# Logits asked for chunk by chunk in the value steps, and inverse row sums stored from their column form

## The chip, the cores and the metric

The kernel runs on one core of a Trainium2 chip. The metric is the device time of one execution in microseconds (us). Before the change three runs took 1028.32, 1027.87 and 1028.21 us; their median is 1028.21.

## The reference

One layer of a decoder trunk over 1024 tokens of width 1024, in float32: a combined projection, a pooling mixer on half of the width, attention with a forgetting gate on the other half (8 heads of 64), an output projection, a layer norm, a squared-relu MLP of width 4096 and a second layer norm. The change lies in the attention:

```python
log_f = jax.nn.log_sigmoid(f_logit)            # per token and head
cf = jnp.cumsum(log_f, axis=-1)
s = einsum('bhqd,bhkd->bhqk', q, k) * HEAD_DIM ** -0.5
s = s + cq[..., :, None] - cf[..., None, :]
s = where(kpos <= qpos, s, NEG_INF)            # causal
p = softmax(s, axis=-1)
out = einsum('bhqk,bhkd->bhqd', p, v)
x = layer_norm(ALPHA * x + concat(pool, attn) @ w_out)
```

## The kernel before, in words

Every float32 product is made from operands split in a high and a low part, so that most products are three matmuls (L82, L83, L84). The program runs in stages: the projections for values and gate, pooling and the first queries and keys; then attention (about 100 to 330 us), into whose steps the next projections and the first output projections are mixed as filling; then the rest of the output projection; then the MLP, which reads its weights from DRAM and is a dense run of matmuls (L796, L1136) to the end.

**Units.** Attention works in 32 units `(p, e, m)`: head pair p, head e of the pair, and block m of 256 queries, which is two row blocks of 128 queries. For the first three pairs a head's units come as m = 3, 2, 1, 0; for the last pair m rises and the two heads alternate. A unit has two halves. `att_probs` makes the probabilities of a unit: per row block the logits in chunks of up to 512 keys (two matmuls at L375 into a PSUM bank with the tag `s`, of which there are three), a fused add-and-minimum on VectorE that takes the chunk out of the bank (L380, with a running minimum `nm`), and one exponential over the row block on ScalarE (L382), which also leaves the row sums in `rsum`. A row block with up to 512 keys has one chunk, one with more has two; units with m = 2 or 3 thus have four chunks, those with m = 0 or 1 two. `att_values` uses the probabilities: for each of its m + 1 value steps `jp` it turns four (in the last step three) 128x128 blocks by TensorE transposes (L405, into a bank with the tag `pt`, of which there are two), splits them out of the bank (L406 on ScalarE, L407 on VectorE) and, up to two steps later, multiplies them with the values (L420, into halves of the one `pv` bank). After a unit's last product the result is added up in a tile `mx` (L429, L430; the `U` tiles, two slots) and stored to `mix_dram` by SyncE's queue (L432, L434).

**What sets the order.** `att_probs` is a generator, and `att_values` of one unit drives `att_probs` of the next (`ahead`). Before the change the generator yields once per row block. It is asked for one row block in step `jp == 0`, and for all that is left in step `min(m, (m + 1) // 2 + 1)`, which is the last step for every m. After each step `fillstep` lets in a share of the filling. A scheduler then places the instructions on each engine; each engine works in its order.

**Inverse row sums.** When the sums of a head (first three pairs) or of a row pair (last pair) are there, VectorE takes their reciprocal into a column tile `ri` of 128 partitions and 8 or 2 columns (L443). `row_scales`, called at the unit's last product, turns it: a TensorE transpose into a `pt` bank (L466), a copy to a row tile (L468, ScalarE), and a store to `rin_dram` (L469, SyncE's queue) of 8 or 2 rows of 512 bytes. It happens 6 times with 8 columns and 8 times with 2. `attention_part` later loads the inverses broadcast over 64 partitions (L580) and multiplies them in (L584).

Of the kernel before, what the change touches and what calls it, by code (L numbers as in the profile page):

```python
# [14 lines left out]
P = 128  # L15
S = 1024
D = 1024
NT = S // P
# [18 lines left out]
def trunk(ctx, tc, xT, xn, wuqk, wvf, bf, poolw, pscale, wout, g1, b1, w1, w2, g2, b2, out):  # L37
# [5 lines left out]
    nc = tc.nc  # L43
# [7 lines left out]
    def slot(tag, shape, dt=F32R):  # L51
        uid[0] += 1
        return sb.tile([P] + list(shape), dt, tag=tag, bufs=NBUF[tag], name=f"{tag}{uid[0]}")

    def small(shape, tag, dt=F32, bufs=1, pool=None):
        uid[0] += 1
        return (pool or sb).tile(list(shape), dt, tag=tag, bufs=bufs, name=f"{tag}_{uid[0]}")
# [5 lines left out]
    def bank(tag=None):  # L63
        uid[0] += 1
        if tag is None:
            tag = CYCLE[rr[0] % 8]
            rr[0] += 1
        return ps.tile([P, CH], F32, tag=tag, bufs=PBUF[tag], name=f"{tag}{uid[0]}")
# [18 lines left out]
    ident = small([P, P], "ident")  # L87
# [17 lines left out]
    rin_dram = dr.tile([NH, S], F32, name="rin_dram")  # L105
# [96 lines left out]
    for t in range(4, NT):  # L202
        for half in range(2):
            b = bank()[:, 0:VW]
# [53 lines left out]
    def run(gen):  # L258
        for _ in gen:
            pass  # L260
# [86 lines left out]
    def gate_row(h):  # L347
        if h not in gate_rows:
            gate_rows[h] = slot("A", [S], F32)
            rsum[h] = small([P, NT], "rsum", bufs=3)  # L350
            nc.sync.dma_start(gate_rows[h], ncf_dram[h : h + 1, :].to_broadcast([P, S]))

    def att_probs(p, e, m, prob):


        KS, q = QK[p][0][e], QK[p][1]
        h = 2 * p + e
        gate_row(h)
        nb = gate_rows[h]
        falling = p < NPAIR - 1  # L360
        for i in (2 * m + 1, 2 * m) if falling else (2 * m, 2 * m + 1):
            nk = (i + 1) * P
            n2 = nk if m % 2 else 256 * (m + 1)
            qs = slice(i * P, (i + 1) * P)
            if falling:
                nc.gpsimd.tensor_tensor(nb[:, qs], nb[:, qs], maskb, ALU.add)
            prob[i % 2] = pt = slot("A", [S], F32)
            top = BIG
            for a in range(0, nk, CH):
                b = min(n2, a + CH)  # L370
                diag = not falling and a <= i * P < b
                sp = bank("s")[:, : b - a]
                for n in range(2):
                    rows = q[n, e, i // 4][:, i % 4 * P : (i % 4 + 1) * P]
                    nc.tensor.matmul(sp, rows, KS[:, a:b], start=n == 0, stop=n == 1 and not diag)  # L375
                if diag:
                    nc.tensor.matmul(sp[:, i * P - a : (i + 1) * P - a], identb, maskb, start=False, stop=True)
                b = min(nk, b)
                nm = small([P, 1], "nm", bufs=8)
                nc.vector.tensor_tensor_reduce(pt[:, a:b], sp[:, : b - a], nb[:, a:b], -1.0, top, ALU.add, ALU.min, nm)  # L380
                top = nm
            nc.scalar.activation(pt[:, :nk], pt[:, :nk], AF.Exp, bias=nm, scale=-1.0, accum_out=rsum[h][:, i : i + 1])  # L382
            yield

    def att_values(p, e, m, prob, ahead):
        h = 2 * p + e
        rows = slice(e * HD, (e + 1) * HD)
        orow = slice((1 - e) * HD, (2 - e) * HD)
        if "values" not in fill:
            fill["values"] = bank("pv")  # L390
        ov = fill["values"][:, 256 * fill["half"] : 256 * fill["half"] + 256]
        fill["half"] = 1 - fill["half"]

        def turned(jp):
            tp = bank("pt")
            tt = slot("A", [2, CH])
            if jp < m:
                blocks = [(jj * 256 + ii * P, 2 * jp + jj, ii) for jj in range(2) for ii in range(2)]
                ev = slice(0, CH)
            else:  # L400
                blocks = [(P, 2 * jp + 1, 1), (2 * P, 2 * jp, 0), (3 * P, 2 * jp, 1)]
                ev = slice(P, CH)
                nc.gpsimd.memset(tt[:, :, 0:P].bitcast(F32), 0.0)
            for col, j, ii in blocks:
                fill["turn"] = nc.tensor.transpose(tp[:, col : col + P], prob[ii][:, j * P : (j + 1) * P], ident).ins  # L405
            nc.scalar.copy(tt[:, 0, ev], tp[:, ev])  # L406
            fill["sub"] = nc.vector.tensor_tensor(tt[:, 1, ev], tp[:, ev], tt[:, 0, ev].bitcast(F32), ALU.subtract).ins  # L407
            return tt

        def multiply(jp, tt):  # L410
            mov = ((0, 256), (256, CH)) if jp < m else ((256, CH), (0, 256))
            with ExitStack() as order:
                for behind in (fill["piece"], fill["turn"]):
                    if behind:
                        order.enter_context(tc.issue_after(behind))
                for s in range(2):
                    for jj in range(2):
                        j = 2 * jp + jj
                        a, b = mov[jj]
                        nc.tensor.matmul(  # L420
                            ov, V[j][:, h].rearrange("p s d -> p (s d)"), tt[:, s, a:b],
                            start=(j == 0 and s == 0), stop=(j == 2 * m + 1 and s == 1),
                        )
            if jp == m:
                last = p == NPAIR - 1
                if not last or e == 0:
                    fill["mx"] = slot("U", [256], F32)
                mx = fill["mx"]
                nc.scalar.copy(mx[rows], ov[orow])  # L429
                nc.vector.tensor_tensor(mx[rows], ov[rows], mx[rows], ALU.add)  # L430
                if not last:
                    nc.sync.dma_start(mix_dram[m, rows, NG + p, :], mx[rows])  # L432
                elif e:
                    nc.sync.dma_start(mix_dram[m, :, NG + p, :], mx)  # L434
                if last:
                    row_scales(h, 2 * m, 2)
                elif m == 0:
                    row_scales(h, 0, NT)

        if p == NPAIR - 1 or m == 0:  # L440
            ri = small([P, NT], "ri", bufs=3)
            i, n = (2 * m, 2) if p == NPAIR - 1 else (0, NT)
            nc.vector.reciprocal(ri[:, :n], rsum[h][:, i : i + n])  # L443
            inverse[h, i] = ri

        for jp in range(m + 1):
            left.append((multiply, jp, turned(jp)))
            if jp == 0:
                fill["last"] = fill["sub"]
                next(ahead, None)  # L450
            if jp == min(m, (m + 1) // 2 + 1):
                run(ahead)
            fillstep()
            values(2)

    left, inverse = [], {}

    def values(n):
        while len(left) > n:
            step, jp, tt = left.pop(0)  # L460
            step(jp, tt)

    def row_scales(h, i, n):
        ri = inverse.pop((h, i))
        tp = bank("pt")
        nc.tensor.transpose(tp[0:n, 0:P], ri[:, :n], ident)  # L466
        row = small([NT, P], "row")
        nc.scalar.copy(row[0:n], tp[0:n, 0:P])  # L468
        nc.sync.dma_start(rin_dram[h, i * P : (i + n) * P].rearrange("(i q) -> i q", q=P), row[0:n])  # L469

    g0 = qk_proj(0)
    for _ in range(2 * KT):
# [222 lines left out]
    def fillstep():  # L695
        fill["credit"] += fill["rate"]
        while fill["credit"] >= 1.0:
            fill["credit"] -= 1.0
            piece = next(fill["gen"], None)
            if piece and fill["pieces"] < 8:  # L700
                fill["piece"], fill["pieces"] = piece, fill["pieces"] + 1
# [4 lines left out]
    for n, unit in enumerate(order):  # L706
# [20 lines left out]
        if n % 8 == 7 and n + 1 < len(order):  # L727
            run(gen)
    att_values(*pend, iter(()))
    values(0)  # L730
    run(gen)
# [603 lines left out]
```

## Time and profile before

| | |
|---|---|
| median of three runs | 1028.21 us |
| profiled execution, its own time | 1028.26 us |
| span of its instructions | 1026.5 us |
| TensorE matmuls (PE) | busy 1013.1 us, 99% |
| TensorE weight loads (PEld) | 843.8 us, 82% |
| VectorE (DVE) | 754.4 us, 73% |
| ScalarE (ACT) | 513.3 us, 50% |
| GpSimdE (POOL) | 153.6 us, 15% |
| granted TensorE clock | 0.997 |

Busy time is the union of the intervals of an engine's instructions. The end of a matmul is modelled, and matmuls overlap; what a matmul costs is therefore read from the start of one to the start of the next. In a timeline row stand the start and the length in us, engine, line, operation, tiles, shapes and how many were merged; in brackets the idle time before it and what ended it. In a row of waits stand the total in us, how often, and the longest.

### The profile page before, as it was taken

Reading aid. Unit: us, or ns where it says so; the run is one execution under the profiler, and the core shown is the slowest. Engines: PE = TensorE matmul, PEld = TensorE weight load, DVE = VectorE, ACT = ScalarE, POOL = GpSimd, SP = SyncE. Lnnn points to the kernel's source line nnn. Section 1 sums busy time; section 2 is a strip of 40 time slices with the busy share of each in tenths; the row PEclk is TensorE's granted clock in tenths of the full one; section 3 lists DMA queues with packets and bytes.
Section 4 is the critical chain, followed back from the end, with each engine's and each line's share of the span. In section 5 each row is a group of like instructions: output and inputs, shape, how many; then the busy total and the mean of one; then the engine's idle time right before and its main releaser. Section 6 shows DMA issues by size and latency. Waiting matters only on the chain.

```text
span 1026.5 us, 14095 instructions
## 1 busy us (share of the span) xinstructions
PE 1013.1 (99%) x4976; PEld 843.8 (82%) x4976; DVE 754.4 (73%) x1303; ACT 513.3 (50%) x825; POOL 153.6 (15%) x269
## 2 busy tenths in 40 slices
PE   9999999999999999999999999999999999999996
PEld 9988888888788888888888888888888888888884
DVE  6576677777868798989888787798866565565547
ACT  5423665666755333678667667669521121221152
POOL 0200111111110032112221221220000000000057
PEclk9999999999999999999999999999999999999998
DMA  9702211111682633259676675665999888878753
GB/s 354 285 28 88 97 52 53 34 48 52 205 290 91 188 141 103 82 185 362 235 273 236 241 275 222 251 260 191 350 309 289 298 265 264 289 237 274 231 179 123
DMA packets 113399, 206.17 MB, mean 201 GB/s; under 512 B 9576, under 2 KB 77608, under 8 KB 113328
## 3 DMA queue, kind: packets, MB, share of 16 engines
q1 hardware_dynamic: 94176, 136.97, 40.7%
q0 software_dynamic: 18720, 67.64, 17.0%
q8 instruction: 39, 0.64, 0.2%
q10 hardware_dynamic: 432, 0.66, 0.2%
q14 instruction: 32, 0.26, 0.1%
HBM read 132.29 MB, written 72.94 MB: 200 GB/s over the span
## 4 chain that ended last, share of the span: by engine, by line
PE 58%; DVE 2%; issue 0%; ACT 0%; DVEq 0%
PE s L1136 17%; PE s L796 11%; PE pv L1136 9%; PE mm L796 7%; PE pt L796 7%; PE pv L796 4%; PE pt L1136 2%; PE mm L1136 2%; DVE B L71 0%; DVE bns L639 0%; DVE A L664 0%; DVE pt L661 0%; DVE pt L1153 0%; DVE A L870 0%; DVE pv L1153 0%
## 5 line engine op out<-in xcount | busy, mean ns | idle before, releaser
L71 ACT CAST B<-S 128x1024 fp32r<-128x1024 f32 (+1 forms) x78 | 67.6, 880 | 162.9 <-DMA S<-in_w_dram 85.0
L796 PE MATMUL s<-B,Q 128*128 128x512 f32 x492 | 116.4, 389 | 0.2 <-ACT B L71 0.2
L796 PEld LDWEIGHTS s<-B,Q 128*128 128x128 f32 x492 | 92.3, 188 | 19.7 <-ACT B L71 0.6
L71 DVE TENSOR_TENSOR B<-S,B 128x1024 fp32r<-128x1024 f32 (+1 forms) x78 | 78.0, 1008 | 37.7 <-ACT B L71 37.6
L1136 PE MATMUL s<-B,Q 128*128 128x512 f32 x402 | 98.5, 390 | 0.0
L1136 PEld LDWEIGHTS s<-B,Q 128*128 128x128 f32 x402 | 75.5, 188 | 16.5
L71 ACT CAST Q<-S 128x1024 fp32r<-128x1024 f32 (+2 forms) x54 | 55.7, 1031 | 63.6 <-PE s L796 17.0
L921 POOL DMA_DIRECT2D hid_dram<-A x90 | 48.1, 538 | 218.1 <-ACT A L918 171.5
L1136 PE MATMUL s<-B,A 128*128 128x512 f32 x321 | 80.3, 394 | 0.0
L71 DVE TENSOR_TENSOR Q<-S,Q 128x1024 fp32r<-128x1024 f32 (+2 forms) x54 | 65.5, 1213 | 12.8 <-ACT Q L71 12.6
L796 PE MATMUL pt<-B,Q 128*128 128x512 f32 x312 | 74.6, 389 | 0.0
L1136 PEld LDWEIGHTS s<-B,A 128*128 128x128 f32 x321 | 60.4, 188 | 13.9
L796 PE MATMUL mm<-B,Q 128*128 128x512 f32 x300 | 71.6, 389 | 0.0
L382 ACT ACTIVATE A<-A,nm 128x1024 f32<-128x1024 f32 (+7 forms) x64 | 49.7, 777 | 42.0 <-DVE nm L380 41.9
L407 DVE TENSOR_TENSOR A<-pt,A 128x512 fp32r<-128x512 f32 (+1 forms) x80 | 50.1, 633 | 25.1 <-ACT A L406 24.3
L796 PEld LDWEIGHTS pt<-B,Q 128*128 128x128 f32 x312 | 58.5, 188 | 12.1
L796 PEld LDWEIGHTS mm<-B,Q 128*128 128x128 f32 x300 | 56.3, 188 | 11.7
L919 DVE TENSOR_TENSOR A<-A,A 128x1024 f32<-128x1024 f32 x45 | 53.6, 1218 | 0.0
L406 ACT CAST A<-pt 128x512 fp32r<-128x512 f32 (+1 forms) x80 | 42.4, 541 | 22.2 <-PE pt L405 21.6
L375 PE MATMUL s<-Q,Q 128*128 128x512 f32 (+2 forms) x192 | 52.2, 368 | 1.3 <-DVE nm L380 1.3
L420 PE MATMUL pv<-A,B 128*128 128x256 f32 x320 | 53.1, 289 | 0.2 <-DVE U L430 0.2
L420 PEld LDWEIGHTS pv<-A,B 128*128 128x128 f32 x320 | 45.8, 189 | 6.4 <-DVE U L430 3.2
(432 smaller groups left out, 2290.1 us busy)
## 6 DMA issues: line engine op xcount, KB each, us to landing
hid_dram<-A POOLq DMA_DIRECT2D x105, 512.0 KB, 3.8
S<-in_w_dram SPq DMA_DIRECT2D x62, 512.0 KB, 4.4
Q<-hid_dram SPq DMA_DIRECT2D x98, 256.0 KB, 5.3
A<-hid_dram SPq DMA_DIRECT2D x82, 256.0 KB, 5.3
S<-in_wuqk_dram SPq DMA_DIRECT2D x12, 512.0 KB, 4.7
wo_dram<-Q POOLq DMA_DIRECT2D x10, 512.0 KB, 4.3
B<-wo_dram SPq DMA_DIRECT2D x10, 512.0 KB, 6.8
Q<-hid_dram SPq DMA_DIRECT2D x39, 128.0 KB, 3.2
```

What stands on the lines that cost most here:

```text
L71: return nc.scalar.copy(hi, src).ins, nc.vector.tensor_tensor(lo, src, hi.bitcast(F32), ALU.subtract).ins
L375: nc.tensor.matmul(sp, rows, KS[:, a:b], start=n == 0, stop=n == 1 and not diag)
L382: nc.scalar.activation(pt[:, :nk], pt[:, :nk], AF.Exp, bias=nm, scale=-1.0, accum_out=rsum[h][:, i : i + 1])
L406: nc.scalar.copy(tt[:, 0, ev], tp[:, ev])
L407: fill["sub"] = nc.vector.tensor_tensor(tt[:, 1, ev], tp[:, ev], tt[:, 0, ev].bitcast(F32), ALU.subtract).ins
L420: nc.tensor.matmul(ov, V[j][:, h].rearrange("p s d -> p (s d)"), tt[:, s, a:b], start=(j == 0 and s == 0), stop=(j == 2 * m + 1 and s == 1),)
L796: nc.tensor.matmul(dst, b[x][:, k], A[a][y][:, k], start=first and k == 0 and i == 0, stop=k == H - 1 and i == 2, skip_group_check=not first,)
L919: nc.vector.tensor_tensor(x, x, hi.bitcast(F32), ALU.subtract)
L921: nc.gpsimd.dma_start(hid_dram[self.u, :, i, AT[name] : AT[name] + 2 * CH], part.rearrange("p q n t -> p (q n t)"))
L1136: nc.tensor.matmul(dst, h[:, p_], w[q_], start=first and u == self.us[0] and j == 0, stop=u == self.us[-1] and j == 2, skip_group_check=no ...
```

## The change

`att_probs` now yields after each chunk that is not the last of its row block, besides the yield after the exponential. `att_values` asks for one such piece in every step but its last, and for all that is left in the last one. For a unit of four chunks that follows one with m = 3 the pieces fall 1, 1, 1, 1 instead of 2, 0, 0, 2; after m = 2 they fall 1, 1, 2 instead of 2, 0, 2; after m = 1 (once, in the last pair) 1, 3 instead of 2, 2; after m = 0 all fall in the one step, as before. A unit of two chunks after m = 2 is done in the first two steps instead of the first and the third.

`row_scales` is gone, and with it the 14 transposes, the 14 copies and the `row` tile. The reciprocal is followed at once by a store of the column tile itself, with the same addresses in `rin_dram`; `ri` has four slots instead of three. Lines move: up to L382 the numbers stay as they were, then L382 becomes L384, L405 becomes L407, L420 becomes L422, L432 becomes L434, L443 becomes L441 with its store at L442, and lines behind `row_scales` are lower by 9.

```diff
                 nc.vector.tensor_tensor_reduce(pt[:, a:b], sp[:, : b - a], nb[:, a:b], -1.0, top, ALU.add, ALU.min, nm)
                 top = nm
+                if b < nk:
+                    yield
             nc.scalar.activation(pt[:, :nk], pt[:, :nk], AF.Exp, bias=nm, scale=-1.0, accum_out=rsum[h][:, i : i + 1])
             yield
...
-                if last:
-                    row_scales(h, 2 * m, 2)
-                elif m == 0:
-                    row_scales(h, 0, NT)

         if p == NPAIR - 1 or m == 0:
-            ri = small([P, NT], "ri", bufs=3)
             i, n = (2 * m, 2) if p == NPAIR - 1 else (0, NT)
+            ri = small([P, NT], "ri", bufs=4)
             nc.vector.reciprocal(ri[:, :n], rsum[h][:, i : i + n])
-            inverse[h, i] = ri
+            nc.sync.dma_start(rin_dram[h, i * P : (i + n) * P].rearrange("(i q) -> q i", q=P), ri[:, :n])

         for jp in range(m + 1):
             left.append((multiply, jp, turned(jp)))
             if jp == 0:
                 fill["last"] = fill["sub"]
+            if jp < m:
                 next(ahead, None)
-            if jp == min(m, (m + 1) // 2 + 1):
+            else:
                 run(ahead)
             fillstep()
             values(2)
...
-    def row_scales(h, i, n):
-        ri = inverse.pop((h, i))
-        tp = bank("pt")
-        nc.tensor.transpose(tp[0:n, 0:P], ri[:, :n], ident)
-        row = small([NT, P], "row")
-        nc.scalar.copy(row[0:n], tp[0:n, 0:P])
-        nc.sync.dma_start(rin_dram[h, i * P : (i + n) * P].rearrange("(i q) -> i q", q=P), row[0:n])
```

The scheduler's result at three places. In these rows stand the line, the operation, the tile written, the tiles read, and the shape; the number behind a tile's name tells one tile from another.

**TensorE, first head, first unit's value steps (m = 3).** The piece of the difference where the two orders first part. `s_1227` is the first chunk of the next unit's first row block, `s_1232` (before) and `s_1243` (now) its second, `mm_1209` filling.

```order
 L375 MATMUL s_1227<-Q_975,Q_977 128x512
 L82 MATMUL mm_1209<-B_157,B_1206 128x512
-L375 MATMUL s_1232<-Q_975,Q_976 128x256
-L375 MATMUL s_1232<-Q_975,Q_977 128x256
 L83 MATMUL mm_1209<-B_157,B_1206 128x512
 L84 MATMUL mm_1209<-B_157,B_1206 128x512
+L375 MATMUL s_1243<-Q_975,Q_976 128x256
+L375 MATMUL s_1243<-Q_975,Q_977 128x256
```

The second chunk moved back by two matmuls of filling.

**TensorE, fifth head, first unit's value steps.** Before, with the transpose of the fourth head's inverse sums (`pt_2450`) between filling (`mm`), a logit chunk (`s_2519`) and the turning of probabilities (`pt_2455`):

```order
L375 MATMUL s_2488<-Q_1738,Q_1739 128x256
L375 MATMUL s_2488<-Q_1738,Q_1740 128x256
L82 MATMUL mm_2505<-B_390,B_2346 128x512
L83 MATMUL mm_2505<-B_390,B_2346 128x512
L466 MATMUL pt_2450<-ident_63,ri_2353 8x128
L84 MATMUL mm_2505<-B_390,B_2346 128x512
L375 MATMUL s_2519<-Q_1738,Q_1739 128x512
L405 MATMUL pt_2455<-ident_63,A_2377 128x128
L405 MATMUL pt_2455<-ident_63,A_2364 128x128
L420 MATMUL pv_1216<-A_2356,B_417 128x256 x4
```

And now, at the same place:

```order
L375 MATMUL s_2472<-Q_1734,Q_1735 128x256
L375 MATMUL s_2472<-Q_1734,Q_1736 128x256
L82 MATMUL mm_2489<-B_390,B_2334 128x512
L83 MATMUL mm_2489<-B_390,B_2334 128x512
L407 MATMUL pt_2439<-ident_63,A_2366 128x128
L407 MATMUL pt_2439<-ident_63,A_2353 128x128
```

The transpose of the sums is gone, and the next turning of probabilities stands where it stood.

**SyncE's queue, second head.** Before, with the store of the row tile (`row_1852`) between the results of the head's last two units (`U_1827` and `U_1846`; `U_1723` is that of its unit m = 2). `S` is a weight load, `A<-ncf_dram` the gate row of a later head:

```order
L432 DMA mix_dram<-U_1723 64x256
L75 DMA S_2941<-in_wuqk_dram 128x1024
L432 DMA mix_dram<-U_1827 64x256
L469 DMA rin_dram<-row_1852 8x128
L432 DMA mix_dram<-U_1846 64x256
L351 DMA A_1974<-ncf_dram 128x1024
```

And now, from the result of the head's first unit on (`U_1648`; `U_1719` is that of m = 2):

```order
L434 DMA mix_dram<-U_1648 64x256
L442 DMA rin_dram<-ri_1749 128x8x1
L434 DMA mix_dram<-U_1719 64x256
L75 DMA S_2921<-in_wuqk_dram 128x1024
L434 DMA mix_dram<-U_1818 64x256
L434 DMA mix_dram<-U_1843 64x256
L351 DMA A_1966<-ncf_dram 128x1024
```

The store of the sums moved ahead of two results and one weight load, and has 128 by 8 by 1 elements instead of 8 rows of 128.

More of the change, by code (lines that the diff above doesn't have):

```diff
@@ L454, in att_values @@
             values(2)
-    left, inverse = [], {}
+    left = []
     def values(n):
```

## The prediction

> **What bounds the kernel now.** I read the page's busy times first, then the windows by stage, then the timeline of TensorE around the instructions that go, then the waits of TensorE's two queues.
>
> ```profile
> PE 1013.1 (99%) x4976; PEld 843.8 (82%) x4976; DVE 754.4 (73%) x1303; ACT 513.3 (50%) x825; POOL 153.6 (15%) x269
> ...
> 100.00:352.00 252.00, 249.84 (x1424) 207.45 (x1424) 186.70 (x441) 153.90 (x322) 35.09 (x90) 1.00 0.34 110
> 440.00:640.00 200.00, 200.00 (x884) 165.60 (x883) 166.36 (x208) 140.75 (x176) 42.74 (x77) 1.00 0.69 260
> 640.00:1000.00 360.00, 360.00 (x1572) 294.69 (x1571) 237.19 (x335) 131.71 (x178) 27.91 (x35) 1.00 0.80 263
> ```
>
> In a window's row stand the window, its length, then the busy time and count of PE, PEld, DVE, ACT and POOL, the granted clock, the DMA share and GB/s. TensorE is the bound everywhere: in attention (100 to 352 us) it is busy for 249.84 of 252.00 us, at a granted clock of 1.00, and behind attention for 200.00 of 200.00 and 360.00 of 360.00 us. So what TensorE saves in attention is not caught by a slower engine or a transfer further on; it arrives at the end whole. And what the change takes from ScalarE and VectorE is worth nothing by itself, since ACT has 153.90 of 252.00 us of work there. Since matmuls overlap, the busy time hides small losses; these I read from start to start.
>
> **The transposes of the sums that go.** The second of them, in the timeline (start, length, engine, line, operation, tiles):
>
> ```profile
> 171.44 0.40 PE L82 MATMUL mm<-B,B 128*128 128x512 f32 x1
> 171.68 0.27 PE L466 MATMUL pt<-ident,ri 128*8 128x128 f32 x1
> 171.71 0.48 PE L83 MATMUL mm<-B,B 128*128 128x512 f32 x1
> 172.02 0.39 PE L84 MATMUL mm<-B,B 128*128 128x512 f32 x1
> 172.26 0.40 PE L375 MATMUL s<-Q,Q 128*128 128x512 f32 x1
> ...
> L466 PE MATMUL pt<-ident,ri x14: 270/272/275, 143.3 to 329.9; 128*2 128x128 f32 x8, 128*8 128x128 f32 x6
> ```
>
> A matmul of 512 columns takes 0.23 to 0.24 us from its start to the next (172.02 to 172.26). The transpose takes 0.03 us (171.68 to 171.71), and the matmul behind it 0.31 us instead of 0.23 (171.71 to 172.02). So one costs TensorE 0.03 + 0.08 = 0.11 us, whatever the 0.27 us of its own row say, and the 14 of them 14 x 0.11 = 1.5 us. Nothing takes their place on TensorE.
>
> **The waits that they cause.** The transpose of the sums occupies one of the two `pt` banks until ScalarE has copied it out. At the fourth head's sums:
>
> ```profile
> 222.46 0.40 PE L83 MATMUL mm<-B,B 128*128 128x512 f32 x1
> 222.69 0.28 PE L466 MATMUL pt<-ident,ri 128*8 128x128 f32 x1
> 222.72 0.48 PE L84 MATMUL mm<-B,B 128*128 128x512 f32 x1
> 223.07 0.49 PE L375 MATMUL s<-Q,Q 128*128 128x512 f32 x1
> 223.70 0.33 PE L405 MATMUL pt<-ident,A 128*128 128x128 f32 x1
> ...
> 223.69 0.14 PEld L405 LDWEIGHTS pt<-ident,A 128*128 128x128 f32 x1 [0.44 <-ACT row L468]
> ...
> 221.93 0.69 DVE L407 TENSOR_TENSOR A<-pt,A 128x512 fp32r<-128x512 f32 x1 [2.13 <-ACT A L406]
> ...
> 223.53 0.69 DVE L407 TENSOR_TENSOR A<-pt,A 128x512 fp32r<-128x512 f32 x1
> ```
>
> The next turning of probabilities (L405) waits 0.44 us for the copy L468. From 223.07 to 223.70 are 0.63 us where 0.23 would do: 0.40 us of the 0.44 are lost to TensorE. Without the sums the turning would take the bank that L407 emptied at 221.93 + 0.69 = 222.62, and would not wait. All such waits together, and those on the other releasers of attention:
>
> ```profile
> PEld s L375 <- DVE nm L380: 4.6, 10, 0.9
> PEld pt L405 <- ACT A L382: 2.5, 9, 0.4
> PEld pt L405 <- ACT row L468: 2.3, 6, 0.6
> PEld pt L466 <- DVE A L407: 1.4, 6, 0.2
> ...
> PE s L375 <- DVE nm L380: 1.3, 4, 0.5
> PE pt L405 <- ACT row L468: 0.3, 1, 0.3
> ```
>
> Waits for `row` add up to 2.3 + 0.3 = 2.6 us in seven cases. The bounds are 0 (each is replaced by a wait for the bank's new holder) and 2.6. The one above lost nine tenths; of the short ones up to 0.23 us lies under the matmul that still streams. I take 1.6. The 1.4 us that the transposes of the sums wait themselves I count as nothing: at 222.46 to 222.69 the distance is the usual 0.23.
>
> **The chunks spread over the steps.** Ten units change with four chunks: the six whose values have m = 3 in the first three pairs, and four of the last pair. The chunks wait for a free `s` bank, that is for L380: 4.6 + 1.3 = 5.9 us in 14 cases. But the largest of these are where all four chunks stand in the one step of an m = 0 unit, and there the order stays:
>
> ```profile
> 214.91 0.39 PE L82 MATMUL mm<-B,B 128*128 128x512 f32 x1
> 215.14 0.39 PE L83 MATMUL mm<-B,B 128*128 128x512 f32 x1
> 216.02 0.62 PE L375 MATMUL s<-Q,Q 128*128 128x384 f32 x2 [0.49 <-DVE nm L380]
> ```
>
> 0.88 us from 215.14 to 216.02 instead of 0.23: 0.65 lost. There are five such places, at most 5 x 0.65 = 3.3 us that remain; 5.9 - 3.3 = 2.6 us is the most that spreading can win. Against it stands that the first row block's exponential now comes one step later, closer to the second's, and turning waits for exponentials already (2.5 us in 9 cases, at most 0.4 each): ten units by 0.4 us are up to 4.0 us lost. Bounds -2.6 and +4.0; I take 0, because the last chunk of a unit, on which the next unit's turning depends, stays in the same step in nearly all of them.
>
> **The store in column form.** Neighbours in a column tile's row go to addresses 512 bytes apart, and neighbours in DRAM lie on different partitions; so nothing joins, and a store of 8 columns is 1024 pieces of 4 bytes, 64 for each of 16 engines. The trace of before has no such store. The nearest rows:
>
> ```profile
> q1 hardware_dynamic: 94176, 136.97, 40.7%
> q0 software_dynamic: 18720, 67.64, 17.0%
> ...
> DMA to landing us min/median/max: 2.0/2.3/3.1
> ...
> L302 SPq DMA_DIRECT2D mix_dram<-A x3: 377/377/377, 99.5 to 116.4; - x3
> ...
> 185.53 0.20 DVE L443 RECIPROCAL ri<-rsum 128x8 f32<-128x8 f32 x1
> 186.39 0.42 DVE L430 TENSOR_TENSOR U<-pv,U 64x256 f32<-64x256 f32 x1 [0.66 <-ACT U L429]
> ...
> 186.83 0.45 SPq L432 DMA_DIRECT2D mix_dram<-U  x1
> ...
> 197.69 0.37 ACT L429 COPY U<-pv 64x256 f32<-64x256 f32 x1
> ```
>
> A piece costs 0.407 x 16 x 1026.5 / 94176 = 71 ns on SyncE's queue at the mean, and 0.170 x 16 x 1026.5 / 18720 = 149 ns at the dearest, for pieces hundreds of times larger. 64 of them are 4.5 to 9.5 us; the lower bound is nothing. The issue is taken at about 0.4 us (L302 issues 512 rows in 377 ns). On SyncE the store waits for the reciprocal, and behind it stand the results of units m = 2 and m = 1 and a weight load. It makes none of them late by its wait: the reciprocal starts at 185.53, and the result that follows is added up at 186.39 only. If its pieces are slow, the result's store (186.83) lands later than 2.3 us after. What is late next is the copy two units on, which needs that `U` slot, at 197.69, and TensorE behind it for the `pv` half. The cover is 197.69 - 186.83 - 2.3 = 8.6 us. I take the mean price, 4.5 us, which lies under it: 0. The eight stores of 2 columns have a quarter of the pieces.
>
> The Trainium skill (DMA: Bandwidth & Descriptors, Rules for kernel authors) speaks against this edit: it says that a strided last dimension becomes one descriptor per element, and that a transpose by a plain DMA with a rearranged pattern is 19 times dearer than the hardware's. By that figure, on the 2.3 us of a result's store, a column store would take an estimated 44 us, 33 beyond cover and landing, and six of them would add some 198 us. No run here shows it yet; its own place is the rival on the store, below.
>
> **Sum.** Against the profiled execution, 1028.26 us (span 1026.5 and 1.8 around it): -1.5 - 1.6 + 0 + 0 = -3.1, so 1025.2 us. The median of the runs, 1028.21, lies 0.05 lower, which changes nothing.
>
> **Rivals.**
>
> *The banks are short anyway.* With the sums gone, the turnings move closer together and wait for L407 of the tile before instead: in the rows above the second `pt` bank is empty at 223.53 + 0.69 = 224.22, not earlier. For it: those L405 waits exist on L407's side too. Against it: the first bank was free 0.7 us before the turning that waited. Only the 1.5 us arrive: 1026.7. Chance 0.27.
>
> *Late exponentials.* In the ten units the next turning waits for the exponential, each time the longest wait seen, 0.4 us, and then also finds the banks empty, so that the 1.6 us are not had: -1.5 + 4.0 = +2.5, so 1030.7. It decides from 3.1 / 10 = 0.31 us for each unit on. For it: waits on L382 are already the second largest. Against it: only one of four pieces moves behind where it stood. Chance 0.09.
>
> *A slow column store.* At the dearest price 9.5 us stand against a cover of 8.6; 0.9 us six times are 5.4, less 3.1: +2.3, so 1030.5. It decides from 8.6 / 64 = 134 ns for each piece on. For it: nothing here shows pieces of 4 bytes written one by one. Against it: the pieces that set these prices are far larger. Chance 0.04.
>
> *Spreading pays in full.* -3.1 - 2.6 = -5.7, so 1022.5. For it: the chunks stand apart in the new order, with two matmuls of filling more between the first pair. Against it: where the loss is largest nothing moves. Chance 0.12.
>
> **How the numbers follow.** My forecast has 0.48: 1025.2 us. With the rivals' chances: the measurement tells a difference from 0.2% on, 2.06 us, so faster means under 1026.15 and slower over 1030.3. Faster: 0.44 of the forecast, 0.12 and 0.05 of the bank rival, 0.61. Slower: 0.07 of the late exponentials and all 0.04 of the store, 0.11. The rest, 0.28, is no change. The range goes down to the full gain of spreading, 1022.4, and up to where the late exponentials have eaten the gain, 1028.9.
>
> **What would show it.** In the profile after, L466, L468 and waits for `row` are gone, TensorE's matmuls in the program are 14 fewer, and the waits of L407 (the old L405) on their banks stay under 1.0 us in place of 2.6. The waits of L375 for `nm` still stand at the m = 0 units, 3 us or more in sum. The 1024-piece store lands within 7 us (4.5 + 2.3). Wrong would be the forecast if the waits of L407 on the exponential grew from 2.5 us to over 5, if the copies L431 sat idle for a store, or if a new wait stood behind 352 us.

## The result and the profile after

The changed kernel takes 1042.81 us (median of 4 runs, 1041.31 to 1044.3) where the kernel before takes 1028.26 us (1027.87 to 1030.22) beside it: a ratio of 1.0138 [1.0116, 1.0159], so 14.6 us slower. The forecast was 1025.2 us. The profiled execution took 1044.3 us, with a span of 1042.5 us, 16.0 us more than the profiled execution before.

The page of the changed kernel, busy times and granted clock by slices, then the DMA packets:

```profile
PE 1016.0 (97%) x4962; PEld 846.3 (81%) x4962; DVE 755.2 (72%) x1303; ACT 512.8 (49%) x811; POOL 153.8 (15%) x269
...
PEclk9999999999898999999999999999999999999998
...
DMA packets 121687, 206.17 MB, mean 198 GB/s; under 512 B 17928, under 2 KB 85896, under 8 KB 121616
```

TensorE's share fell from 99% to 97% though it has 14 instructions fewer. In two slices of the attention (261 to 287 us and 313 to 339 us, each slice being 26.06 us) the granted clock has the digit 8, where the kernel before has 9. The bytes are those of before, but there are thousands of packets of under 512 B more. Where the time was lost, by windows of the changed kernel:

```profile
100.00:368.00 268.00, 252.72 (x1403) 209.33 (x1402) 186.25 (x439) 151.72 (x307) 35.37 (x90) 0.97 0.42 103
368.00:1042.00 674.00, 664.47 (x2943) 546.90 (x2941) 503.49 (x728) 318.21 (x429) 110.72 (x144) 1.00 0.69 237
```

and the matching window of the kernel before:

```profile
352.00:1026.00 674.00, 664.55 (x2938) 546.25 (x2936) 502.25 (x726) 317.18 (x429) 110.90 (x144) 1.00 0.68 237
```

Counted from the end, the last 674 us are alike: TensorE is busy for 664.47 and 664.55 us. The whole 16 us went into attention, where TensorE is now busy for 252.72 of 268.00 us and its mean clock is 0.97. The waits of TensorE and of its weight loads, changed kernel:

```profile
PE pv L422 <- DVE U L432: 7.1, 3, 3.9
PE mm L82 <- DVE B L612: 4.9, 1, 4.9
PE s L375 <- DVE nm L380: 1.6, 4, 0.5
...
PEld pv L422 <- DVE U L432: 11.2, 12, 4.4
PEld pt L407 <- ACT A L384: 3.9, 8, 1.9
```

The waits for `row` are gone, as they had to be. The waits of the value products (L422) for the addition that empties their bank (L432) have grown: for the weight loads from 3.2 us in all, 0.6 us at the longest, to 11.2 us and 4.4. New is one of 4.9 us for the residual rows (L612). VectorE, which is waited for, isn't slow there; it stands behind transfers, as the rows below show. The store itself, by its line:

```profile
L442 SPq DMA_DIRECT2D rin_dram<-ri x14: 359/377/932, 133.6 to 340.1; - x14
...
DMA to landing us min/median/max: 10.5/11.9/13.3
```

It is issued in 0.38 us and lands after 10.5 to 13.3 us, as far as the profile has its landing, which is for 4 of the 14; the forecast had 7. The first of the 14 in the timeline, with what stands behind it (SyncE's queue, ScalarE, TensorE):

```profile
133.59 0.37 SPq L442 DMA_DIRECT2D rin_dram<-ri  x1
134.35 0.46 SPq L434 DMA_DIRECT2D mix_dram<-U  x1
...
146.45 0.37 ACT L431 COPY U<-pv 64x256 f32<-64x256 f32 x1 [3.87 <-DMA mix_dram<-U]
...
147.32 0.74 PE L422 MATMUL pv<-A,B 128*128 128x256 f32 x4 [2.29 <-DVE U L432]
```

and the window in between:

```profile
140.00:144.00 4.00, 4.00 (x30) 3.55 (x29) 3.79 (x9) 1.54 (x3) 0.31 (x2) 1.00 0.00 0
```

The result's store, issued at 134.35 behind the column store, lands at 146.45: after 12.1 us, where such a store landed in 2.3 us before. The copy that needs its `U` slot waits 3.87 us for it, and TensorE 2.29 us for the copy. The window's row says what happens meanwhile: from 140 to 144 us the DMA share is 0.00 and nothing moves at 0 GB/s, though the result's store has been issued and has not landed.

### The profile page after: what moved, and what is told of

The parts are those of the page before. It is cut to its first block, busy times and chain, and to the rows that moved or that the text cites. A ratio compares the mean times of both kernels' runs of the same rounds, so it can differ in the third digit from the quotient of the medians.

```text
span 1042.5 us, 14055 instructions
## 1 busy us (share of the span) xinstructions
PE 1016.0 (97%) x4962; PEld 846.3 (81%) x4962; DVE 755.2 (72%) x1303; ACT 512.8 (49%) x811; POOL 153.8 (15%) x269
## 4 chain that ended last, share of the span: by engine, by line
PE 57%; DVE 2%; issue 0%; ACT 0%; DVEq 0%
PE s L1127 16%; PE s L787 10%; PE pv L1127 8%; PE pt L787 7%; PE mm L787 7%; PE pv L787 4%; PE pt L1127 2%; PE mm L1127 2%; DVE B L71 0%; DVE bns L630 0%; DVE A L655 0%; DVE pt L652 0%; DVE pt L1144 0%; DVE A L861 0%; DVE pv L1144 0%
## 5 line engine op out<-in xcount | busy, mean ns | idle before, releaser
L787 PEld LDWEIGHTS pt<-B,Q 128*128 128x128 f32 x312 | 58.5, 188 | 12.1
L787 PEld LDWEIGHTS mm<-B,Q 128*128 128x128 f32 x300 | 56.3, 188 | 11.7
L409 DVE TENSOR_TENSOR A<-pt,A 128x512 fp32r<-128x512 f32 (+1 forms) x80 | 50.4, 634 | 17.8 <-ACT A L408 17.3
L384 ACT ACTIVATE A<-A,nm 128x1024 f32<-128x1024 f32 (+7 forms) x64 | 49.8, 777 | 24.8 <-DVE nm L380 24.1
L422 PE MATMUL pv<-A,B 128*128 128x256 f32 x320 | 54.0, 293 | 7.3 <-DVE U L432 7.1
L422 PEld LDWEIGHTS pv<-A,B 128*128 128x128 f32 x320 | 46.9, 192 | 15.2 <-DVE U L432 11.2
L375 PE MATMUL s<-Q,Q 128*128 128x512 f32 (+2 forms) x192 | 54.9, 376 | 1.6 <-DVE nm L380 1.6
```

What stands on the lines that cost most here:

```text
L422: nc.tensor.matmul(ov, V[j][:, h].rearrange("p s d -> p (s d)"), tt[:, s, a:b], start=(j == 0 and s == 0), stop=(j == 2 * m + 1 and s == 1),)
L787: nc.tensor.matmul(dst, b[x][:, k], A[a][y][:, k], start=first and k == 0 and i == 0, stop=k == H - 1 and i == 2, skip_group_check=not first,)
```

## The experiments

**Each half of the change alone.**

```diff
 # chunks alone: row_scales, its transposes and its row stores stay
+                if b < nk:
+                    yield
...
+            if jp < m:
                 next(ahead, None)
-            if jp == min(m, (m + 1) // 2 + 1):
+            else:
```

```diff
 # store alone: the old order of asking stays
+            nc.sync.dma_start(rin_dram[h, i * P : (i + n) * P].rearrange("(i q) -> q i", q=P), ri[:, :n])
...
-                if last:
-                    row_scales(h, 2 * m, 2)
-                elif m == 0:
-                    row_scales(h, 0, NT)
```

> Only the chunk-by-chunk asking; the turned row form of the sums and its store as before. Theory S (the column store is the whole loss): no loss here, 1026 to 1030 us. Rival C (the new order of the chunks puts TensorE into waits): most of the 14.5 us are here already, 1037 to 1043 us.

> Only the column store; the row blocks asked for as before. Theory S: 1040 to 1046 us, with waits of TensorE for the value products' bank and for the output projection. Rival C: 1024 to 1027 us, the transposes' own 1.5 us and their waits given back.

The chunks alone: 1027.0 us, ratio 0.9989 [0.998, 0.9998]. The store alone: 1047.47 us, ratio 1.0177 [1.0155, 1.0199]. So the order of the chunks wins about 1.3 us, and the store is more than the whole loss; alone it lies a little above the 1040 to 1046 us expected for it, and 4.7 us above the whole change. The waits of the weight loads with the chunks alone say how the new order wins:

```profile
PEld s L375 <- DVE nm L380: 4.6, 9, 0.9
...
PEld pt L407 <- ACT A L384: 1.9, 7, 0.6
...
PEld pt L407 <- ACT row L471: 0.7, 2, 0.4
```

The waits for `nm`, which spreading was to shorten, are the same 4.6 us. What shrank are the waits for the row copies, 2.3 to 0.7 us. The late exponentials did not come: the waits for L384 fell from 2.5 to 1.9 us.

**The store on another queue.** The result's store stands behind the column store on SyncE's queue. Is it the order on the queue that holds it?

```diff
-            nc.sync.dma_start(rin_dram[h, i * P : (i + n) * P].rearrange("(i q) -> q i", q=P), ri[:, :n])
+            nc.scalar.dma_start(rin_dram[h, i * P : (i + n) * P].rearrange("(i q) -> q i", q=P), ri[:, :n])
```

and the same with `nc.gpsimd`.

> The whole change, but the column stores are issued from ScalarE's queue instead of SyncE's. Theory S1 (what is queued behind the store on SyncE's own queue lands late: results, weights, residual rows): gone, 1024 to 1029 us, and results land in 2 to 3 us again. Rival S2 (the 4-byte pieces hold the 16 DMA engines or the memory, whatever queue they came from): still 1036 us or more.

> The whole change, but the column stores are issued from GpSimdE's queue. S1: 1024 to 1031 us, where what is lost comes from GpSimdE's own work (mask additions) waiting behind the issue. S2: 1036 us or more.

ScalarE's queue: 1065.2 us, ratio 1.0354 [1.034, 1.0368]. GpSimd's queue: 1060.35 us, 1.0302 [1.0281, 1.0323]. Both are slower than the change as it is. With ScalarE's queue, the same place in the timeline:

```profile
133.95 0.38 ACTq L442 DMA_DIRECT2D rin_dram<-ri  x1
...
135.22 0.46 SPq L434 DMA_DIRECT2D mix_dram<-U  x1
...
146.88 0.37 ACT L431 COPY U<-pv 64x256 f32<-64x256 f32 x1 [3.95 <-DMA mix_dram<-U]
```

The result's store is now on a queue of its own and still needs 11.7 us (135.22 to 146.88). So it isn't queue order alone; the column store holds the transfers of other queues too. These two kernels lose some 20 us more than the change. With ScalarE's queue TensorE waits 19.8 us in six cases for the additions (L432), where the change has 7.1 us in three: the same kind of stall, more often. Why it comes more often is open.

**What about the pieces is dear?** The changed kernel's DMA issues, by size (at the end the median us to landing):

```profile
rin_dram<-ri SPq DMA_DIRECT2D x8, 1.0 KB, 13.2
...
rin_dram<-ri SPq DMA_DIRECT2D x6, 4.0 KB, 10.5
```

The 8 stores of 256 pieces land in 13.2 us, the 6 of 1024 pieces in 10.5 us: four times the pieces, no more time. Each median rests on two landings alone, and the two small stores stand close to others. But small stores that come 12 us or more after the one ahead of them don't take a quarter of the time either: 11.0 us in the kernel with the store alone (issued at 330.91 us), 12.1 us with ScalarE's queue (at 328.71 us). So a price for each piece, on which both the forecast and the rival on the store rested, can't be it. Four kernels add one more store of the reciprocals' tile to the kernel before, each with other addresses; nobody reads what it writes. (`ri` has four slots in the three that write to DRAM; the added tiles' allocations are left out here.)

```diff
             nc.vector.reciprocal(ri[:, :n], rsum[h][:, i : i + n])
             inverse[h, i] = ri
 # 512 B apart, more: [P, NT, P]
+            nc.sync.dma_start(more.pop()[:, :n, 0:1], ri[:, :n].rearrange("q (i o) -> q i o", o=1))
 # side by side as in the change, more: [NT * P]
+            nc.sync.dma_start(more.pop()[0 : n * P].rearrange("(i q) -> q i", q=P), ri[:, :n])
 # one piece per partition, more: [P, NT]
+            nc.sync.dma_start(more.pop()[:, :n], ri[:, :n])
 # into SBUF, far: [P, NT, 2]
+            nc.sync.dma_start(far[:, :n, 0:1], ri[:, :n].rearrange("q (i o) -> q i o", o=1))
```

> The kernel before, with one store added behind each of the 14 reciprocals: the same 4-byte pieces of the reciprocal tile, on the same queue, but each piece 512 B from the next, into DRAM that nobody reads. The stores of the changed kernel land in 10.5 us with 1024 pieces and in 13.2 us with 256 of them, so the time does not follow the number of pieces, and three theories of what holds them are left. Same-line theory (the 16 pieces that fall into each 64 B of DRAM are written one behind the other, about 0.7 us each, whatever the number of lines): here no two pieces share a line, so the added stores land in 2 to 4 us, the copies wait for no store, ratio 0.999 to 1.004. Every 4-byte write into DRAM is dear: landing 10 to 13 us and ratio 1.012 to 1.022, like the column store alone (1.0177). Every 4-byte piece is dear wherever it goes: the same, 1.012 to 1.022.

> The kernel before, with one store added behind each of the 14 reciprocals, of the very pattern of the change (4-byte pieces, those of neighbouring partitions side by side in DRAM), into DRAM that nobody reads; the row form with its transposes stays and is what the readers get. All theories that blame the store expect the loss back with nothing else changed: landing 10 to 13 us, ratio 1.012 to 1.025 (the column store alone gave 1.0177, without the 14 row stores and transposes). If instead the loss came from readers that wait for the column store (the residual rows' scales at the end of the last pair), nobody reads here, and the ratio is 0.999 to 1.004.

> The kernel before, with one store added behind each of the 14 reciprocals: the same tile and the same 128 partitions, but what a partition holds goes to one place (32 B for the first six heads, 8 B in the last pair, 32 B from one partition to the next), into DRAM that nobody reads. Same-line theory: two pieces share each 64 B, so landing 2 to 4 us, ratio 0.999 to 1.005. Every small piece is dear by its number: 128 in place of 1024 or 256; as the landing of 256 and of 1024 pieces was alike (13.2 and 10.5 us), a theory of pieces that reckons with a fixed 10 us for any store from 128 partitions expects landing 10 us again and ratio 1.012 to 1.022.

> The kernel before, with one transfer added behind each of the 14 reciprocals: the same 4-byte pieces on the same queue, but from SBUF to SBUF, each piece 8 B from the next within its partition; nobody reads them. Same-line theory, and the theory that every 4-byte write into DRAM is dear: landing 2 to 5 us (64 pieces for each of 16 engines at 0.07 us, the mean packet on that queue, is 4.5 us), ratio 0.999 to 1.005. Every 4-byte piece is dear wherever it goes: landing 10 us or more, ratio 1.012 to 1.022.

Ratios: 512 B apart 1.0 [0.9991, 1.001]; side by side 1.0394 [1.0358, 1.0429]; one piece per partition 1.0002 [0.9993, 1.0012]; into SBUF 0.9997 [0.9988, 1.0007]. The added store, 512 B apart (packets of the whole kernel, then its landing):

```profile
DMA packets 121815, 206.20 MB, mean 201 GB/s; under 512 B 17992, under 2 KB 86024, under 8 KB 121744
```

```profile
DMA to landing us min/median/max: 1.9/3.0/5.9
```

Side by side (the number of packets is again 121815), the landing, and then the wait it brings:

```profile
DMA to landing us min/median/max: 8.5/11.9/13.0
```

```profile
PE pv L421 <- DVE U L431: 17.7, 4, 8.0
```

One piece per partition, 32 B from the next:

```profile
DMA to landing us min/median/max: 1.4/2.0/5.8
```

Into SBUF (the last number is the median us to landing):

```profile
far<-ri SPq DMA_DIRECT2D x8, 1.0 KB, 2.5
far<-ri SPq DMA_DIRECT2D x6, 4.0 KB, 2.4
```

This is the clearest pair of the study: the same tile, the same 121815 packets, the same pieces of 4 B, issued at the same point; only the addresses differ, and one costs nothing while the other costs 4%. Neither the number of pieces, nor their size, nor the 128 partitions they come from is dear by itself. Dear is that pieces of 4 B fall close together in DRAM. The neighbours come from different partitions here; no run puts small pieces of one partition side by side, so whether that matters is open. That the added store costs more (1.0394, above the 1.012 to 1.025 expected) than the change's (1.0177 alone) was not settled; the row stores stand behind it there.

**The same arrangement at twice the distance.**

```diff
 # 8 B apart, more: [NT * P, 2]
+            nc.sync.dma_start(more.pop()[0 : n * P, 0:1].rearrange("(i q) o -> q i o", q=P), ri[:, :n].rearrange("q (i o) -> q i o", o=1))
```

> The kernel before, with one store added behind each of the 14 reciprocals: the same 4-byte pieces on the same queue, each 8 B from the next in DRAM, so 8 in place of 16 fall into each 64 B; nobody reads them. Same-line theory with one write behind the other: about half the landing of the pieces side by side (8.5 to 13.0 us, median 11.9), so 4 to 7 us, and as the copies' cover is 8.6 us, a small loss: ratio 1.002 to 1.015. If the hold comes with any two pieces in a line, whatever their number: landing 8 to 13 us, ratio 1.015 to 1.04.

Ratio 1.0088 [1.0074, 1.0102].

```profile
DMA to landing us min/median/max: 4.1/7.3/12.2
```

In both kernels the profile has the landing of three stores alone, and they are the same three, the 9th, 12th and 13th of the 14, each of 256 pieces: 7.3, 12.2 and 4.1 us at 8 B against 11.9, 13.0 and 8.5 us at 4 B. The 13th, which comes 19 us or more after the one ahead of it, takes half, as one write behind the other would give; the 12th has two others within 3.5 us ahead of it and hardly gains. How large the stretch is in which writes queue up these runs don't say: 128 pieces, each 32 B from the next, were free of it. If writes in one stretch go one behind the other and the stretches side by side, then it is no larger than 1 KB, since 256 pieces in 1 KB take about as long as 1024 in 4 KB; that is argued, not shown. The 64 B in the expectations were a supposition.

**The store only for the first six heads.** The order of asking is the new one; in the last pair the row form stays.

```diff
-            inverse[h, i] = ri
+            if p == NPAIR - 1:
+                inverse[h, i] = ri
+            else:
+                nc.sync.dma_start(rin_dram[h].rearrange("(i q) -> q i", q=P), ri)
```

> The changed kernel with the column store only for the first six heads of the phase (1024 pieces each, one store per 26 us); the eight stores of the last pair (256 pieces each) have the row form again, with transposes. The prediction's rival of a slow store counted six overruns of the slot of the results, 5.3 us in all: then the ratio is 1.003 to 1.007, and the last pair, where the column stores stand 4 to 16 us apart and the next phase's rows and weights are loaded, has the larger part of the loss. If the loss goes by pieces (6144 of 8192 are in the first six): 1.009 to 1.013.

1036.42 us, ratio 1.0081 [1.0067, 1.0094]: between the two expectations, 9.4 us over the chunks alone. Not six places lose it but two. The first is the first store, with the stall shown above; the other is the sixth store. The timeline at the first and the waits between 272 and 284 us:

```profile
147.43 0.72 PE L422 MATMUL pv<-A,B 128*128 128x256 f32 x4 [2.22 <-DVE U L432]
```

```profile
PE pv L422 <- DVE U L432: 3.8, 1, 3.8
```

The windows behind that wait:

```profile
280.00:282.00 2.00, 1.88 (x7) 1.68 (x7) 1.97 (x5) 1.62 (x4) 0.95 (x2) 0.50 0.53 131
...
284.00:286.00 2.00, 2.00 (x7) 1.51 (x6) 0.73 (x3) 0.33 (x2) 0.00 (x0) 0.50 0.88 277
```

2.2 us and 3.8 us of standing still, and then, behind the second, 6 us in which the granted clock is 0.50: 3.0 us more. Together 9.0 us, which is the difference of the span from that of the chunks alone (1034.2 and 1025.2 us).

**The same aim without small pieces.** VectorE turns the tile in 32x32 blocks, and the rows go out in pieces of 128 B. (`square` are two tiles of 128x32, set to zero once.)

```diff
-            ri = small([P, NT], "ri", bufs=4)
+            ri, turn = square[h % 2], small([P, 32], "turn", bufs=2)
             nc.vector.reciprocal(ri[:, :n], rsum[h][:, i : i + n])
-            nc.sync.dma_start(rin_dram[h, i * P : (i + n) * P].rearrange("(i q) -> q i", q=P), ri[:, :n])
+            nc.vector.transpose(turn, ri)
+            for b in range(4):
+                nc.sync.dma_start(
+                    rin_dram[h, i * P : (i + n) * P].rearrange("(i b q) -> b i q", b=4, q=32)[b], turn[32 * b : 32 * b + n]
+                )
```

once with the new order of asking, and once with the old:

> The changed kernel with its column store replaced: VectorE turns the reciprocals' tile (128x32, the columns beyond the reciprocals set once to zero) in 32x32 blocks, and four transfers store the turned rows, in pieces of 128 B that share no 64 B with another. No transpose on TensorE, no copy on ScalarE, no 4-byte piece. Same-line theory, and the prediction's terms for what was removed: the order of the chunks gives its 1.1 us (1027.0 alone), the 14 transposes 1.5 us, the waits for the row copies 0 to 2.6 us: 1022.5 to 1025.5 us, ratio 0.9945 to 0.9975; the stores land in 1.5 to 4 us. Rival (the transposes and their waits were never on the path, since the weight loads or the buffers end the same stretch): ratio 0.998 to 0.9995, like the chunk order alone. Rival (any store from the column form holds the transfers, whatever its pieces): 1.01 or more.

> The kernel before with the block transpose on VectorE and its four stores in place of the transposes on TensorE, the row copies and their stores, and with the old order of asking for the chunks. The prediction's first two terms alone: 1.5 us of transposes and 0 to 2.6 us of waits for the row copies: 1024.2 to 1026.8 us from 1028.3, ratio 0.996 to 0.9986. Rival (they were never on the path): 0.999 to 1.001.

New order: 1024.99 us, ratio 0.9967 [0.9954, 0.9979], 3.2 us less than the kernel before beside it (1028.21 us). Old order: 1026.14 us, 0.9978 [0.9969, 0.9987], 2.1 us less. The new block transposes by their line, and the largest waits of the weight loads on the tiles concerned, with the new order:

```profile
L442 DVE STREAM_TRANSPOSE turn<-square x14: 170/211/214, 133.5 to 320.2; 128x32 f32<-128x32 f32 x14
```

```profile
PEld pv L422 <- DVE U L432: 2.2, 6, 0.5
PEld pt L407 <- DVE A L409: 2.0, 7, 0.4
PEld pt L407 <- ACT A L384: 2.0, 7, 0.6
```

14 x 0.21 = 3.0 us on VectorE and 56 issues on SyncE's queue; the view of `turn` shows no instruction that waits for either. With the old order (weight loads' waits):

```profile
PEld pt L405 <- ACT A L382: 4.7, 12, 1.4
...
PEld pt L405 <- DVE A L407: 2.2, 11, 0.3
```

## Why the prediction was wrong

**The step that failed: "I take the mean price, 4.5 us, which lies under it: 0."** The column store's term was 0 and measured 18 to 21 us (store alone 1047.47 against 1026.14 with the same removals and a harmless store: 21.3; the change, 1042.81 against 1024.99: 17.8). Three things are wrong in it.

First, the kind of price. I priced the store by packets, 64 for an engine by 71 to 149 ns, from rows of far larger packets. With the same packets 512 B apart the store lands in 3.0 us at the median and costs nothing, so the low price was even too high for pieces as such. What the sum left out is where they land: side by side they take 11.9 us, and for that time other transfers don't get through. The eight small stores with "a quarter of the pieces" were no faster.

Second, the cover. "The cover is 197.69 - 186.83 - 2.3 = 8.6 us" was read at one head of six. At the first head of the kernel before the store and the copy stood closer:

```profile
135.23 0.47 SPq L432 DMA_DIRECT2D mix_dram<-U  x1
...
144.88 0.37 ACT L429 COPY U<-pv 64x256 f32<-64x256 f32 x1
```

144.88 - 135.23 - 2.3 = 7.4 us, while the result's store there overran by 12.1 - 2.3 = 9.8. In the changed kernel the cover was shorter still: without its wait the copy would have gone at 146.45 - 3.87 = 142.58, so 142.58 - 134.35 - 2.3 = 5.9 us. The copy came 3.9 us late, and TensorE lost 2.29 of them. And the cover was read for the `U` slot alone. The sixth store meets the weights of the output projection. Changed kernel, SyncE's queue, ScalarE and TensorE:

```profile
263.00 0.38 SPq L442 DMA_DIRECT2D rin_dram<-ri  x1
...
267.19 1.20 SPq L548 DMA_DIRECT2D S<-in_wout_dram  x2
...
276.73 1.04 ACT L71 CAST B<-S 128x1024 fp32r<-128x1024 f32 x1 [5.62 <-DMA S<-in_wout_dram]
277.80 0.36 ACT L431 COPY U<-pv 64x256 f32<-64x256 f32 x1
...
279.55 1.22 PE L422 MATMUL pv<-A,B 128*128 128x256 f32 x4 [3.93 <-DVE U L432]
```

ScalarE waits 5.62 us to round a weight that has not come, and the copy of the result, which waits for no transfer by its own row, stands behind it on the same engine. VectorE's part of the rounding (277.81 us, 1.23 us long) then stands ahead of the addition (279.06 us) that TensorE waits for. I named what is queued behind the store on SyncE; what is queued on ScalarE behind the users of those transfers I did not. In the last pair the residual rows are caught in the same way:

```profile
305.62 0.34 SPq L524 DMA_DIRECT2D B<-in_xn_dram  x1
306.90 1.67 SPq L442 DMA_DIRECT2D rin_dram<-ri  x2
...
320.12 0.69 DVE L612 SCALAR_TENSOR_TENSOR B<-B,mm 128x512 f32<-128x512 f32 x1 [5.32 <-DMA B<-in_xn_dram]
...
320.86 0.79 PE L82 MATMUL mm<-B,Q 128*128 128x512 f32 x1 [4.94 <-DVE B L612]
```

The rows were asked for ahead of the store, and are late all the same: 5.32 us for VectorE, 4.94 for TensorE. Where the last pair keeps the row form (the store only for the first six heads), TensorE has no such wait.

Third, the clock. The prediction took the granted clock of 1.00 as given. Changed kernel, a window in the first stall, then the end of the stall from 275.6 us with what follows it, and the same for that from 315.9 us:

```profile
144.00:147.00 3.00, 1.02 (x7) 0.69 (x6) 0.66 (x3) 0.53 (x2) 0.85 (x2) 1.00 0.69 152
...
278.70:285.50 6.80, 5.73 (x16) 3.88 (x16) 4.14 (x9) 2.94 (x7) 1.54 (x3) 0.50 0.61 83
...
319.70:326.40 6.70, 5.54 (x16) 4.25 (x17) 6.10 (x14) 1.07 (x2) 0.00 (x0) 0.50 0.88 199
```

A stall of 2.29 us leaves the clock at 1.00. In the stalls of 3.93 and 4.94 us it falls to 0.50 before they end, and it stays there until 6.0 and 5.6 us after their ends; that costs 3.0 and 2.9 us more. But the length of a stall doesn't settle it. In the kernel with the store on GpSimd's queue the first stall is as short as that of the change, and the clock fell behind it (TensorE's row, then the window):

```profile
147.60 1.22 PE L422 MATMUL pv<-A,B 128*128 128x256 f32 x4 [2.28 <-DVE U L432]
```

```profile
147.60:151.00 3.40, 3.40 (x12) 3.11 (x13) 1.51 (x4) 2.21 (x6) 0.00 (x0) 0.50 0.10 29
```

The Trainium skill (TensorE: Matmul & The Clock Gate, Part 1: The HAM clock gate) says that an idle window of about 3.4 us halves TensorE's clock until it has been busy for about as long. The three stalls of the change agree with the first half of that, the one of 2.28 us does not, and in the change the return took longer, 6.0 and 5.6 us. The measurement decides: a stall of over 2 us can already cost the clock.

The loss in the profile is then: stalls of 2.3, 3.9, 1.2, 0.8 and 4.9 us (those of 1.2 and 0.8 on L384 and L432 between 286 and 302 us), 13.1 in all, and what the low clock took, window by window its length times what the clock lacks of 1.00: 3.0 us from 279.5 to 287 and 2.9 us from 320.8 to 327. That is 19.0 of the 19.9 us by which the span exceeds that of the block transpose, 1022.6 us.

**The rival of a slow store** was right in its side and its mechanism as far as it went (the result's store late, the `U` slot late, the value products waiting), with 0.04 and 1030.5 us. It was under-priced by the same three points: six overruns of 0.9 us, where the six heads lost 9.0 us at two places, and nothing for the last pair, where the other stores cost the rest. "It decides from 134 ns for each piece on" has no meaning, as the pieces don't set the time. "The pieces that set these prices are far larger" was the argument against it; I should have read it as saying that no row prices this at all, and given the rival more. The range had its own slips: the full gain of spreading ends at 1028.26 - 5.7 = 1022.6, not 1022.4, and a gain that is eaten up leaves 1028.26, not 1028.9.

**The rule against the edit.** A store with the same pieces adds 121815 - 113399 = 8416 packets for its 8192 elements. On this the Trainium skill (DMA: Bandwidth & Descriptors, Rules for kernel authors), with one descriptor for each element of a strided last dimension, agrees with the trace. Its 19 times do not show here: estimated from it were 44 us for a store and 198 us for the kernel; measured are 10.5 to 13.3 us side by side, 3.0 us apart, and 14.6 us for the kernel. The measurement decides; but in its direction that rule was the better guide than my rows.

**The terms that were right, and how.** Transposes and row waits together were to give 1.5 + 1.6 = 3.1 us. Measured, with a harmless store in their place: 2.0 us with the new order (1027.0 to 1024.99) and 2.1 us with the old (1028.21 to 1026.14). If the 1.5 us for the transposes hold, the waits gave 0.5 of the 1.6. The rows of the old order show why: as the waits for `row` (2.6 us) went, those of L405 on L407 rose from 0.7 to 2.2 us and those on the exponential from 2.5 to 4.7 us. The first of these is the rival of the short banks, whose 1026.7 us lies nearer to the 1026.14 measured than the 1025.2 of the two terms in full; I had given it 0.27. The second it did not name.

The spread chunks were set at 0 between -2.6 and +4.0 and measured -1.2 us (1.3 alone, 1.15 between the two block transposes). The rival of the late exponentials is out: with the chunks alone those waits fell. But spreading did not win where its bound was taken from, at the banks `s`: those waits are unchanged, as the prediction said for the m = 0 units. By the rows of waits it won at the row copies (2.3 to 0.7 us) and the exponentials (2.5 to 1.9 us, and 4.7 to 2.0 between the two block transposes).

So the 1025.0 us of the block transpose fall on the forecast of 1025.2 us, but by other terms: 2.0 and 1.2 in place of 3.1 and 0. The sum agreeing does not make its parts right.

**What was to show it.** L466, L468 and the `row` waits gone: yes. 14 matmuls fewer: yes (4976 to 4962). Waits for `nm` of 3 us or more: yes (1.6 us of TensorE and 4.5 of its weight loads). The waits of L407 on their banks under 1.0 us: no, 1.5 us (for L409). A landing within 7 us: no, 10.5 at the least. Of what would make it wrong, the waits on the exponential grew to 3.9 us, not to over 5, and no new wait stands behind attention. But "if the copies L431 sat idle for a store" is what happened: 3.87 us.

## What to carry to other kernels

A store that puts small pieces from many partitions side by side in DRAM is not priced by its packets: it took 10.5 to 13.3 us to land here, held up transfers of its own queue and of others meanwhile, and another issuing engine did not help. Turn the tile on the chip (0.21 us on VectorE for 128x32) so that it goes out in longer runs, each from one partition (128 B here). Where a transfer may come late, look for the shortest cover of all places, and follow it through the in-order engines: what stands behind the instruction that waits for it, and whether TensorE's clock then falls.

## What the runs showed of the hardware that was not expected

The time of such a store does not grow with its pieces (256 in 13.2 us, 1024 in 10.5 us) but with how close they lie: landing 11.9 us at 4 B, 7.3 us at 8 B, 3.0 us at 512 B, 2.0 us for one piece per partition at 32 B, 2.4 to 2.5 us into SBUF (medians, of few landings where the pieces lie close). In the first six heads the pieces at 32 B are 32 B long, so they lie end to end in DRAM and come from different partitions, and still cost nothing; whether it is their size or their number of 128 that makes the difference from the pieces of 4 B no run separates. While such a store lasts, transfers that another queue has issued do not finish either: a result's store on SyncE's queue took 11.7 us beside a column store on ScalarE's. The Trainium skill (DMA: Bandwidth & Descriptors, Back-pressure in remote DMA) tells for transfers between cores that stalled writes stall the other queues of a DMA engine; the runs here look like that for a plain store to DRAM. What in the memory makes neighbouring writes queue up no run shows.
